# Hybrid SSD/attention layer on one Trainium2 core: attention's negated row maxima from one matmul a head and half, and group norm factors spread by transposes

## The chip, the core and the metric

One core of a Trainium2 chip runs the whole layer as one program. The engines work side by side, each through its own stream of instructions: TensorE (PE in the profile; its weight loads are PEld), VectorE (DVE), ScalarE (ACT), GpSimd (POOL) and SyncE (SP, which here issues most of the DMAs). TensorE writes its results to PSUM, in banks of 128 partitions by 512 float32; VectorE and ScalarE read them there. The metric is the device time of one execution in microseconds, the median of several runs. Lower is better.

## The reference

One layer over 1024 tokens of width 1024. Two branches start from the same normed input: a Mamba-2 state-space branch (SSD, 32 heads of 64 in 4 groups) and a latent attention branch (16 heads, 96 wide for queries and keys, 64 for values). Their outputs are gated and added, projected, and a gated MLP with a short causal convolution follows. What the change touches:

```python
# attention, one head: causal softmax over the keys
s = jnp.einsum('bqhd,bkhd->bhqk', qb, k).astype(jnp.float32) * scale
s = jnp.where(qpos[:, None] >= key_pos[None, :], s, -jnp.inf)
p = jax.nn.softmax(s, axis=-1).astype(v.dtype)
...
# end of the SSD branch: an RMS norm within each group of 512 channels
y = y.reshape(b, l, D_INNER) * jax.nn.silu(z)
y = rms_norm(y.reshape(b, l, SSD_GROUPS, D_INNER // SSD_GROUPS),
             norm_g.reshape(SSD_GROUPS, D_INNER // SSD_GROUPS))
```

All of it is float32 at the boundary. The kernel computes the large products in three passes, with each operand split into a rounded part and a remainder (`mm3`, lines 175 to 177).

## The kernel before

**Order.** PE runs its instructions in program order; at the end of the kernel every PE instruction is chained to the one before it. The other engines' streams follow from the order of the program and its dependencies. While attention and the SSD scan run, PE also works through a queue of background projections: `fill()` and `advance()` put a number of background steps, given by a string of digits (`PACE`), between the steps of the foreground. A background step is one `mm3`, three matmuls of 128x128 by 512 columns into the tile `lin`.

**Attention** (lines 528 to 760, 110 to 690 us in the profile). It goes over 8 pairs of heads and 2 halves of 512 queries. For each pair, half and head:

- `qk_transposed` (L605 to L615) puts queries and keys with the head's dimension on partitions: `qh`, `ql`, `kh`, `kl`. They have 97 rows: 96 of the head and one more, which is 1 in the keys and is to hold the negated row maximum in the queries. So the product of keys and queries comes out with the maximum subtracted.
- `maxima` (L617 to L645) works out that maximum beforehand. For each of 4 blocks of 128 queries PE multiplies queries by keys (L627), and DVE takes the row maximum (L629, L632) into `nm`. DVE then writes the 4 columns of maxima, one for each block of queries, into columns 96 to 99 of the tile `mcol` (L637 or L639, `mc` in the profile), whose first 96 columns are zero. Four matmuls (L643) follow: number i takes columns i to i+96 of `mcol` as its stationary operand and the negated identity `nid` as its moving one, so its row 96 is the negated maxima of block i as a row of 128. One ACT copy (L644) takes row 96 of all four, 512 columns, from PSUM to row 96 of `qh`.
- `key_block` (L647 to L665) multiplies 128 keys by the 512 queries, adds the causal mask on the diagonal (L657, DVE), takes exp (L659, ACT) and adds up the sums; `values` (L670) multiplies by V, two key blocks later.

The heads of a pair go through `maxima` step by step in turn (`both`), so the two L643 blocks of a pair stand one after the other in PE's stream, with background steps between them in four of the 16 pairs. The maxima of a pair's second half are computed while the first half's key blocks run, and those of the next pair's first half while the second half's run; the list `SIDE` says how many such side steps go into each gap. The last two side steps during a first half stand just ahead of that half's end; during a second half there are six more gaps behind them.

The tiles named `s` are four PSUM banks that L627, L643, the key blocks and the transposes take in turn.

**SSD** (lines 832 to 968, 790 to 1275 us). It goes over 4 groups and 8 chunks of 128 tokens. `ssd_inputs` starts a chunk with four transposes (L840) and two matmuls (L842, L844). Group norm is in `ssd_finish`, for each group and half: four matmuls (L947) sum the squares over partitions, `rsqrt_mean` (L123 to L125, DVE) makes 4 columns of factors `rr` (`grr` in the profile), and four float32 matmuls (L955) spread them. Number i takes column i, read 128 times, as its stationary operand and the identity as its moving one, so that every partition of the PSUM tile `np_` gets the 128 factors as a row. DVE then multiplies the four channel tiles by it (L958), and they are stored.

Of the kernel before, what the change touches and what calls it, by code (L numbers as in the profile page):

```python
# [10 lines left out]
F32R = mybir.dt.float32r  # L11
I32 = mybir.dt.int32
AF = mybir.ActivationFunctionType
ALU = mybir.AluOpType
# [3 lines left out]
P = 128  # L18
# [54 lines left out]
def tile_hybrid_layer(ctx: ExitStack, tc: tile.TileContext, x, cols, cons, w_main, w_small, w_uq, w_ukv,  # L73
                      w_ssd, w_mla, w_o, w_up, w_down, out, pace=PACE):
    nc = tc.nc
    V, S, G, PE = nc.vector, nc.scalar, nc.gpsimd, nc.tensor
# [20 lines left out]
    ident = cn[:, CC_ID:CC_ID + 128]  # L97
# [10 lines left out]
    def col(c):  # L108
        return cl[:, c:c + 1]

    def hs_(half):
        return slice(half * 512, half * 512 + 512)

    def rsqrt_mean(dst, ss, n):

        w = dst.shape[1]
        v = const.tile([P, 16], F32, name="rsv", bufs=1)[:, 0:w]
        a = const.tile([P, 16], F32, name="rsa", bufs=1)[:, 0:w]
        V.tensor_scalar(v, ss, 1.0 / n, EPS, op0=ALU.mult, op1=ALU.add)
        V.tensor_scalar(dst.bitcast(I32), v.bitcast(I32), 1, None, op0=ALU.logical_shift_right)  # L120
        V.tensor_scalar(dst.bitcast(I32), dst.bitcast(I32), -1.0, float(0x5F3759DF), op0=ALU.mult, op1=ALU.add)
        for _ in range(3):
            V.scalar_tensor_tensor(a, dst, -0.5, v, op0=ALU.mult, op1=ALU.mult)  # L123
            V.tensor_tensor(a, a, dst, op=ALU.mult)
            V.scalar_tensor_tensor(dst, a, 1.5, dst, op0=ALU.add, op1=ALU.mult)  # L125
# [9 lines left out]
    def last(engine):  # L135
        return [ins for ins in nc.cur_bb.bb.instructions if ins.engine == engine][-1].name
# [15 lines left out]
    def split(raw, hi, lo, eng=None):  # L152
        S.copy(hi, raw)  # L153
        (eng or V).tensor_sub(lo, raw, hi.bitcast(F32))  # L154
# [24 lines left out]
    def act_tile():  # L179
        return hp.tile([P, 2, 512], F32R, name="h")  # L180
# [14 lines left out]
    def lin_tile():  # L195
        return pl.tile([P, 512], F32, name="lin")
# [231 lines left out]
    rr = bp.tile([P, 2, NT], F32, name="lrr")  # L428
# [8 lines left out]
    for half in range(2):  # L437
        for b in range(3):
            fill()
            ps = bps.tile([P, 512], F32, name="tps")  # L440
# [49 lines left out]
    for n in range(17, 1, -2):  # L490
# [10 lines left out]
    ps = bps.tile([P, 512], F32, name="tps")  # L501
    PE.matmul(ps[:, 0:256], lhsT=tri, rhs=va, start=True, stop=True)
    S.copy(acum.rearrange("p t h -> p (t h)"), ps[:, 0:256])
    ps = bps.tile([P, 512], F32, name="tps")
# [9 lines left out]
                           op0=ALU.mult, op1=ALU.mult)  # L514
    act_ = bq.tile([HEADS, T], F32, name="act_")
    for half in range(2):
        fill()
        ps = bps.tile([P, 512], F32, name="tps")
# [7 lines left out]
    with tc.tile_pool(name="cp", bufs=2) as cp, tc.tile_pool(name="pss", bufs=4, space=PSUM) as pss, \  # L526
# [6 lines left out]
        nid = cp.tile([P, P], F32R, name="nid", bufs=1)  # L533
        V.tensor_scalar(nid, ident, -1.0, None, op0=ALU.mult)

        mcol = [cp.tile([P, 100], F32R, name=f"mc{hd}", bufs=1) for hd in range(2)]
        for hd in range(2):
            V.tensor_scalar(mcol[hd][:, 0:96], ident[:, 0:96], 0.0, None, op0=ALU.mult)
        npair = MH // 2
        qkv, qkvT = {}, {}  # L540

# [60 lines left out]
        def bank():  # L602
            return pss.tile([P, 512], F32, name="s")
# [13 lines left out]
        def maxima(pr, half, hd):  # L617

            qh = qkvT[pr, half, hd, "q"][0]
            nm = cp.tile([P, 2, 4], F32, name="nm")  # L620
            for i in range(4):
                n = (i + 1) * P
                for j in range(half + 1):
                    kh = qkvT[pr, j, hd, "k"][0]
                    w = n if j == half else 512
                    ps = bank()
                    PE.matmul(ps[:, 0:w], lhsT=qh[0:96, i * P:(i + 1) * P], rhs=kh[0:96, 0:w], start=True, stop=True)  # L627
                    if j == half:
                        V.tensor_tensor_reduce(ps[:, 0:w], ps[:, 0:w], negw[:, 512 - w:512], 1.0, 2 * NEG,  # L629
                                               ALU.add, ALU.max, nm[:, j, i:i + 1])  # L630
                    else:
                        V.tensor_reduce(nm[:, j, i:i + 1], ps[:, 0:w], axis=AX.X, op=ALU.max)  # L632
                if i < 3:
                    yield
            mc = mcol[hd][:, 96:100]
            if half:
                V.tensor_tensor(mc, nm[:, 0, :], nm[:, 1, :], op=ALU.max)  # L637
            else:
                V.tensor_copy(mc, nm[:, 0, :])  # L639
            yield  # L640
            ps = bank()
            for i in range(4):
                PE.matmul(ps[0:97, i * P:(i + 1) * P], lhsT=mcol[hd][:, i:i + 97], rhs=nid, start=True, stop=True)  # L643
            S.copy(qh[96:97, :], ps[96:97, :])  # L644
            yield  # L645

        def key_block(pr, half, j, hd, accs):  # L647
# [49 lines left out]
        def both(pr, half):  # L697
            a, b = maxima(pr, half, 0), maxima(pr, half, 1)
            for _ in range(5):
                for g in (a, b):  # L700
                    next(g, None)
                    yield
# [69 lines left out]
    with tc.tile_pool(name="dp", bufs=2) as dp, tc.tile_pool(name="psx", bufs=1, space=PSUM) as psx, \  # L772
# [137 lines left out]
        def ssd_squares(g, c):  # L910
            if c % 4 == 0:
                sums[g, c // 4] = dp.tile([P, 512], F32, name="sqs")
            sq = dp.tile([P, 4, P], F32, name="sq_", bufs=1)
            S.activation(sq, chan[g][:, :, c * P:(c + 1) * P], AF.Square)
            G.tensor_tensor(sq[:, 0:2, :], sq[:, 0:2, :], sq[:, 2:4, :], op=ALU.add)
            G.tensor_tensor(sums[g, c // 4][:, (c % 4) * P:(c % 4 + 1) * P], sq[:, 0, :], sq[:, 1, :], op=ALU.add)
            squared[0] = behind(None)
# [21 lines left out]
        def ssd_finish(g, half):  # L939

            x, s = chan[g], hs_(half)
            if half:
                ssd_squares(g, NT - 1)
                yield
            np_ = psy.tile([P, 512], F32, name="np_")
            for i in range(4):
                PE.matmul(np_[:, i:i + 1], lhsT=sums[g, half][:, i * P:(i + 1) * P], rhs=ones[:, 0:1],  # L947
                          start=True, stop=True)
            rr = dp.tile([P, 4], F32, name="grr")
            rsqrt_mean(rr, np_[:, 0:4], 512)  # L950
            yield
            yield
            np_ = psy.tile([P, 512], F32, name="np_")
            for i in range(4):
                PE.matmul(np_[:, i * P:(i + 1) * P], lhsT=rr[:, i:i + 1].broadcast_to([P, P]), rhs=ident,  # L955
                          start=True, stop=True)
            for j in range(4):
                V.scalar_tensor_tensor(x[:, j, s], x[:, j, s], col(CG_SSDG + 4 * g + j), np_,  # L958
                                       op0=ALU.mult, op1=ALU.mult)
                r0 = (4 * g + j) * P  # L960
                if g == GROUPS - 1 and half == 0:
                    t = act_tile()
                    split(x[:, j, s], t[:, 0, :], t[:, 1, :])
                    ya0[4 * g + j] = t
                else:
                    nc.sync.dma_start(out=y_d[r0:r0 + P, s], in_=x[:, j, s])
            if half:
                finished[0] = g + 1
            yield
# [97 lines left out]
        for n, _ in enumerate(conv_group(0)):  # L1067
# [3 lines left out]
            if n == 33:  # L1071
                name = last(mybir.EngineType.DVE)
# [7 lines left out]
        for g in range(GROUPS):  # L1080
            if g + 1 < GROUPS:
                background += [conv_group(g + 1), z_tiles(*((12,), (13,), (14, 15))[g])]
            else:
                background += [mla_tiles()]

            advance(8 if g else 14)
            n = (106, 104, 128, 112)[g]
            for u, _ in enumerate(ssd_steps(g)):
                advance((u + 1) * n // 23 - u * n // 23)
                if (u % 2 or u == 0) and fins and next(fins[0], 0) == 0:  # L1090
                    fins.pop(0)
                if u % 3 == 1 and (g < 2 or g == 2 and u < 5):
                    normalize(8 * g + u // 3)
                if u == 14:
                    fins.append(ssd_finish(g, 0))
            fins.append(ssd_finish(g, 1))
            if g + 1 < GROUPS:
                flush(1 if g < 2 else 0)
                later()
                if g == GROUPS - 2:  # L1100
                    z_load((g + 1) * NT)
# [68 lines left out]
    with tc.tile_pool(name="ep", bufs=2) as ep:  # L1170
        x2b = []
        with tc.tile_pool(name="em", bufs=2) as em:
# [33 lines left out]
            for half in range(2):  # L1206
# [6 lines left out]
                for ct in range(8):  # L1213
# [4 lines left out]
                    if half == 0 and ct == 0:  # L1218
                        ps = head[0]
                    else:  # L1220
                        ps = lin_tile()
# [210 lines left out]
        for k in range(1, 9):  # L1432
# [3 lines left out]
            i = (k - 1) % 4  # L1436
# [343 lines left out]
```

## Time and profile before

| | |
|---|---|
| median of 3 runs | 2205.24 us (2204.86 to 2205.38) |
| span of the profiled execution, first to last instruction | 2202.2 us |
| around the span (median less span) | 3.0 us |
| mean granted TensorE clock | 0.996 |
| L643, L955 matmul records | 128, 64 |
| L644 copies on ACT | 32 |

The profile is of one execution. Its page gives the span and no other time for that execution; what lies around the span is therefore taken from the median of the runs. Busy time is the union of the instructions' durations on an engine. PE's matmuls are pipelined, so their durations overlap (a 512-column matmul is shown as 0.39 us, but the next one starts 0.23 us after it): what an instruction costs PE is read from start to start. In the timeline each row has the start, the time that the group takes, engine, line, operation, what is written and read, sizes and count; a bracket at the end gives the idle time before it and what ended it. `128*97` means 128 rows by 97 columns of a stationary operand.

### The profile page before, as it was taken

What the parts mean: (1) busy time and instruction counts of PE and PEld (TensorE: products, weight loads), DVE (VectorE), ACT (ScalarE), POOL (GpSimd) and SP (SyncE); (2) the same over time, 40 slices, a digit from 0 to 9 for tenths busy, and PEclk for the clock granted to TensorE, in tenths of its full rate; (3) what the DMA queues carried; (4) which work ended last, traced back from release to release, by engine and by line L of the source; (5) the groups of instructions that cost most, each with busy time, mean ns of one, the idle gap of its engine ahead of it and who ended that gap; (6) DMA issues with size and microseconds to landing.
All of it is one profiled execution on the core that took longest, in us unless ns stands there. A gap on an engine that the chain in (4) does not pass through costs nothing. (4 is left out here: it accounts for less than half of the span.)

```text
span 2202.2 us, 30596 instructions
## 1 busy us (share of the span) xinstructions
PE 2151.8 (98%) x10972; PEld 1723.4 (78%) x10972; DVE 1446.8 (66%) x2567; ACT 1050.6 (48%) x1938; POOL 971.3 (44%) x1049
## 2 busy tenths in 40 slices
PE   8999999999999999999999999999899999999999
PEld 6887777777777887878877888887678888877787
DVE  4466756576664469898877745546876676676763
ACT  5445444554444446565654424324745455554330
POOL 2344424432443237665555311003387777744440
PEclk9999999999999999999999999999999999999999
DMA  4221111101112324554366567452132333248642
GB/s 147 69 69 46 40 53 64 50 35 55 64 44 70 115 77 144 176 171 156 115 221 205 169 208 231 160 175 96 63 112 99 110 106 106 95 143 329 257 158 82
DMA packets 121768, 268.99 MB, mean 122 GB/s; under 512 B 13520, under 2 KB 25744, under 8 KB 121616
## 3 DMA queue, kind: packets, MB, share of 16 engines
q1 hardware_dynamic: 105600, 214.47, 28.9%
q0 software_dynamic: 14528, 49.29, 6.7%
q10 hardware_dynamic: 1488, 3.28, 0.4%
q8 instruction: 86, 1.41, 0.3%
q14 instruction: 66, 0.54, 0.1%
HBM read 201.45 MB, written 65.54 MB: 121 GB/s over the span
## 5 line engine op out<-in xcount | busy, mean ns | idle before, releaser
L175 PE MATMUL lin<-h,whi 128*128 128x512 f32 x1440 | 592.3, 411 | 0.5 <-DVE lt L330 0.5
L177 PE MATMUL lin<-h,wlo 128*128 128x512 f32 x1440 | 564.0, 392 | 0.0
L176 PE MATMUL lin<-h,whi 128*128 128x512 f32 x1440 | 562.7, 391 | 0.0
L175 PEld LDWEIGHTS lin<-h,whi 128*128 128x128 f32 x1440 | 271.0, 188 | 83.0 <-issue 34.1
L177 PEld LDWEIGHTS lin<-h,wlo 128*128 128x128 f32 x1440 | 270.5, 188 | 59.9 <-DVE wlo L154 0.4
L176 PEld LDWEIGHTS lin<-h,whi 128*128 128x128 f32 x1440 | 271.7, 189 | 53.7 <-issue 7.0
L154 POOL TENSOR_TENSOR wlo<-wraw,whi 128x512 fp32r<-128x512 f32 x134 | 192.7, 1455 | 164.4 <-ACT whi L153 163.7
L153 ACT CAST whi<-wraw 128x512 fp32r<-128x512 f32 x232 | 141.0, 619 | 258.1 <-PE lin L176 121.0
L664 POOL TENSOR_TENSOR acc<-acc,e 128x512 f32<-128x512 f32 (+3 forms) x80 | 78.6, 983 | 251.0 <-ACT e L659 227.5
L659 ACT ACTIVATE e<-s 128x512 f32<-128x512 f32 (+1 forms) x192 | 93.6, 493 | 168.9 <-DVE s L657 142.8
L1141 DVE TENSOR_TENSOR xlo<-ur,xhi 128x512 fp32r<-128x512 f32 (+1 forms) x41 | 83.2, 2029 | 61.0 <-ACT xhi L1140 61.0
L154 DVE TENSOR_TENSOR wlo<-wraw,whi 128x512 fp32r<-128x512 f32 x98 | 69.8, 722 | 72.1 <-ACT whi L153 71.7
L850 ACT ACTIVATE seg<-abc,acum 128x128 f32<-128x128 f32 x256 | 80.2, 390 | 51.5 <-PE yp L891 43.9
L175 PE MATMUL dps<-tq,h 128*128 128x512 f32 x242 | 97.5, 403 | 6.6 <-DVE xr L1602 3.3
L176 PE MATMUL dps<-tq,h 128*128 128x512 f32 x242 | 97.6, 403 | 0.8 <-DVE tq L154 0.8
L177 PE MATMUL dps<-tq,h 128*128 128x512 f32 x242 | 97.3, 402 | 0.0
L812 DVE SCALAR_TENSOR_TENSOR xg<-craw,cl,xg 128x1024 f32<-128x1024 f32 x48 | 73.8, 1537 | 27.4 <-ACT xg L810 26.9
L664 DVE TENSOR_TENSOR acc<-acc,e 128x512 f32<-128x512 f32 (+3 forms) x80 | 55.0, 688 | 37.6 <-ACT e L659 37.0
L670 PE MATMUL pv<-e,vt 128*64 128x512 f32 (+3 forms) x384 | 72.9, 498 | 0.0
L154 DVE TENSOR_TENSOR h<-ar,h 128x1024 fp32r<-128x1024 f32 (+1 forms) x35 | 56.7, 1623 | 24.5 <-ACT h L153 24.3
L1217 POOL DMA_DIRECT2D mt<-m_d x16 | 8.6, 540 | 144.6 <-DVE gt L1226 96.8
L629 DVE CUSTOM_DVE_ANT_0 s<-s,negw 128x128 f32<-128x128 f32 (+3 forms) x128 | 62.3, 495 | 13.5 <-PE s L627 13.4
(617 smaller groups left out, 5225.6 us busy)
## 6 DMA issues: line engine op xcount, KB each, us to landing
wraw<-in_w_main SPq DMA_DIRECT2D x112, 256.0 KB
ur<-in_w_up SPq DMA_DIRECT2D x44, 512.0 KB
ar<-f_d SPq DMA_DIRECT2D x34, 512.0 KB
abc<-ac_d POOLq DMA_DIRECT2D x32, 512.0 KB, 5.2
wraw<-in_w_ssd SPq DMA_DIRECT2D x64, 256.0 KB
f_d<-wraw POOLq DMA_DIRECT2D x33, 256.0 KB, 2.4
g_d<-lt SPq DMA_DIRECT2D x32, 256.0 KB
z_d<-lt SPq DMA_DIRECT2D x32, 256.0 KB
```

Source lines behind the costliest of these rows:

```text
L153: S.copy(hi, raw)
L154: (eng or V).tensor_sub(lo, raw, hi.bitcast(F32))
L175: PE.matmul(ps, lhsT=ah, rhs=bh, start=first, stop=False, **more)
L176: PE.matmul(ps, lhsT=ah, rhs=bl, start=False, stop=False, **more)
L177: PE.matmul(ps, lhsT=al, rhs=bh, start=False, stop=last, **more)
L629: V.tensor_tensor_reduce(ps[:, 0:w], ps[:, 0:w], negw[:, 512 - w:512], 1.0, 2 * NEG, ALU.add, ALU.max, nm[:, j, i:i + 1])
L659: S.activation(e[:, c0:512], ps[:, 0:w], AF.Exp)
L664: (V if hd else G).tensor_tensor(accs[hd][:, c0:512], accs[hd][:, c0:512], e[:, c0:512], op=ALU.add)
L670: PE.matmul(pv[hd * 64:(hd + 1) * 64, c0:512], lhsT=vt[:, j, hd * 64:(hd + 1) * 64], rhs=es[hd][:, c0:512], start=first, stop=last)
L812: V.scalar_tensor_tensor(c, raw[:, k:k + T], col(cw + k), c, op0=ALU.mult, op1=ALU.add)
L850: S.activation(seg[:, hd, :], abc[:, hd, :], AF.Relu, bias=acum[:, c, 8 * g + hd:8 * g + hd + 1], scale=-1.0)
L1141: eng.tensor_sub(lo, r, hi.bitcast(F32))
```

## The change

Two edits, both on PE's way.

1. `mcol` becomes 128 columns wide and is zeroed as a whole. The 4 columns of maxima go to columns 0, 32, 64 and 96. One matmul with the whole tile as stationary operand gives rows 0, 32, 64 and 96 of its result, the negated maxima of the four blocks of queries. Four ACT copies, each from one of these partitions, 128 columns, fill row 96 of `qh`.
2. The four matmuls that spread the group norm factors become four PE transposes of the same broadcast column.

```diff
-        mcol = [cp.tile([P, 100], F32R, name=f"mc{hd}", bufs=1) for hd in range(2)]
+        mcol = [cp.tile([P, P], F32R, name=f"mc{hd}", bufs=1) for hd in range(2)]
         for hd in range(2):
-            V.tensor_scalar(mcol[hd][:, 0:96], ident[:, 0:96], 0.0, None, op0=ALU.mult)
+            V.tensor_scalar(mcol[hd], ident, 0.0, None, op0=ALU.mult)
...
-            mc = mcol[hd][:, 96:100]
+            mc = mcol[hd][:, 0:P:32]
             if half:
                 V.tensor_tensor(mc, nm[:, 0, :], nm[:, 1, :], op=ALU.max)
             else:
                 V.tensor_copy(mc, nm[:, 0, :])
             yield
             ps = bank()
+            PE.matmul(ps[:, 0:P], lhsT=mcol[hd], rhs=nid, start=True, stop=True)
             for i in range(4):
-                PE.matmul(ps[0:97, i * P:(i + 1) * P], lhsT=mcol[hd][:, i:i + 97], rhs=nid, start=True, stop=True)
-            S.copy(qh[96:97, :], ps[96:97, :])
+                S.copy(qh[96:97, i * P:(i + 1) * P], ps[32 * i:32 * i + 1, 0:P])
             yield
...
             np_ = psy.tile([P, 512], F32, name="np_")
             for i in range(4):
-                PE.matmul(np_[:, i * P:(i + 1) * P], lhsT=rr[:, i:i + 1].broadcast_to([P, P]), rhs=ident,
-                          start=True, stop=True)
+                PE.transpose(np_[:, i * P:(i + 1) * P], rr[:, i:i + 1].broadcast_to([P, P]), ident)
```

## The prediction

> **What bounds the kernel now.** I read the engine row of the page first, then the table by stretches of the two stages that are touched, and then the timeline around the edited lines.
>
> ```profile
> PE 2151.8 (98%) x10972; PEld 1723.4 (78%) x10972; DVE 1446.8 (66%) x2567; ACT 1050.6 (48%) x1938; POOL 971.3 (44%) x1049
> 110.00:690.00 580.00, 569.39 (x3191) 440.17 (x3189) 371.30 (x1025) 278.02 (x628) 228.54 (x384) 1.00 0.16 52
> 790.00:1275.00 485.00, 479.54 (x2896) 385.32 (x2895) 399.23 (x635) 273.29 (x522) 263.34 (x248) 1.00 0.51 165
> ```
>
> In the stretch rows the columns are length, then busy time of PE, PEld, DVE, ACT and POOL, then granted clock, DMA share and GB/s. PE is busy for 569.4 of 580 us while attention runs and for 479.5 of 485 us in the state-space stage (SSD), at full clock; DMA is busy for 16% and 51%. PE issues in program order, so a microsecond of PE taken out of either stage shortens the run by a microsecond, unless PE then waits for what it did not have to wait for.
>
> **What leaves PE: the maxima.** The pairs of blocks L643 (head 0, head 1) appear in two shapes: eight matmuls in one row, or four and four with a triple of background matmuls between.
>
> ```profile
> 384.58 0.39 PE L177 MATMUL lin<-h,wlo 128*128 128x512 f32 x1
> 384.81 0.82 PE L643 MATMUL s<-nid,mc 128*97 128x128 f32 x8
> 385.38 1.06 ACT L644 CAST qh<-s 1x512 fp32r<-1x512 f32 x2 [0.37 <-PE s L643]
> 385.98 0.40 PE L177 MATMUL lin<-h,wlo 128*128 128x512 f32 x1
> 386.22 0.40 PE L175 MATMUL s<-qh,kh 97*128 97x512 f32 x1
> ```
> ```profile
> 309.12 0.39 PE L177 MATMUL lin<-h,wlo 128*128 128x512 f32 x1
> 309.36 0.48 PE L643 MATMUL s<-nid,mc 128*97 128x128 f32 x4
> 309.67 0.45 PE L175 MATMUL lin<-h,whi 128*128 128x512 f32 x1
> 310.19 0.40 PE L177 MATMUL lin<-h,wlo 128*128 128x512 f32 x1
> ```
> ```profile
> 882.39 0.39 PE L175 MATMUL lin<-h,whi 128*128 128x512 f32 x1
> 882.62 0.39 PE L176 MATMUL lin<-h,whi 128*128 128x512 f32 x1
> 882.84 0.39 PE L177 MATMUL lin<-h,wlo 128*128 128x512 f32 x1
> 883.07 1.05 PE L955 MATMUL np__8996<-cn,grr 128*128 128x128 f32 x8
> 883.96 0.60 PE L840 MATMUL xp<-cn,xg 128*128 128x128 f32 x4
> 884.39 0.39 PE L842 MATMUL sp<-chan 128*128 128x128 f32 x2
> ```
>
> Durations overlap, so I use starts. A 512-column background step is 0.23 us (882.39, 882.62, 882.84, 883.07). From L177 to the next L177 there are three such steps, 0.68 us; with eight L643 between it is 385.98-384.58 = 1.40, so eight cost 0.72; with four, 310.19-309.12 = 1.07, so four cost 0.39. The difference, 0.33 for four, is 0.083 us for each. Of the 32 blocks, 12 pairs are of the first shape and 4 of the second. After the change a pair is two matmuls. The edge of a block stays: 0.39-3x0.083 = 0.14 for one matmul, and 0.22 for two. The new stationary tile has 128 columns, not 97; no row shows that form with 128 moving columns alone, and the nearest rows are these 0.083 and the 0.11 us of a transpose with 128 (L840, 884.39-883.96 = 0.43 for four). I take 0.02 more for each block, nearly the whole of that difference: 0.16 for one, 0.24 for two. So a pair of the first shape saves 0.48 us and one of the second 0.46, about 0.25 in the first block and 0.23 in the second; 12x0.48+4x0.46 = 7.6 us, and 8.0 without the 0.02.
>
> The Trainium skill ("TensorE: Matmul & The Clock Gate", LDWEIGHTS) says that a weight load takes its column count over 1.2 GHz, however many rows it has; that speaks against the edit a little, as 97 columns become 128. As an estimate by that page, 81 ns become 107 ns. The rows give 83 ns a matmul with 97 columns, close to it, and by the rule the edit would save 4x81-107 = 217 ns a block, 6.9 us in all.
>
> **Where this is lost again before head 1's block.** Head 1's matmul needs its own maxima from DVE.
>
> ```profile
> 161.15 0.39 PE L177 MATMUL lin<-h,wlo 128*128 128x512 f32 x1
> 161.20 0.47 DVE L637 TENSOR_TENSOR mc<-nm 128x4 fp32r<-128x4 f32 x1
> 161.38 0.28 ACT L659 ACTIVATE e<-s 128x128 f32<-128x128 f32 x1 [1.49 <-DVE s L657]
> 161.38 0.90 PE L643 MATMUL s<-nid,mc 128*97 128x128 f32 x8
> 161.95 1.06 ACT L644 CAST qh<-s 1x512 fp32r<-1x512 f32 x2 [0.30 <-PE s L643]
> 162.63 0.40 PE L177 MATMUL lin<-h,wlo 128*128 128x512 f32 x1
> 162.87 0.40 PE L175 MATMUL s<-qh,kh 97*128 97x512 f32 x1
> ```
> ```profile
> 503.81 0.17 DVE L639 CAST mc<-nm 128x4 fp32r<-128x4 f32 x1
> 504.12 0.53 PE L643 MATMUL s<-nid,mc 128*97 128x128 f32 x4 [0.40 <-DVE mc L639]
> ```
>
> At 161 the second `mc` ends at 161.67, and four first-head matmuls of 0.083 have just gone by (161.38 plus 0.33): remove three of them, and PE waits that 0.25 us. At 504 it waits already. Going through the 16 pairs in the same way, six are like these two (the first and the last of them are shown): the first block's 0.25 is lost. Three more have the second `mc` only 0.2 to 0.3 us ahead and lose 0.3 together. That takes 6x0.25+0.3 = 1.8 from 7.6 and leaves 5.8. DVE's work is upstream and does not change: the strided write of `mc` has as many elements, and the wider zeroing at the start of attention is two instructions once.
>
> **What is added on ACT: four copies for one.** 32 copies of 512 columns become 128 of 128 columns, on one partition each. No row has 1x128; the nearest in length are 128x128 from PSUM.
>
> ```profile
> 165.54 0.27 ACT L567 COPY vt<-s 128x128 f32<-128x128 f32 x1 [0.43 <-DVE qk L566]
> 165.71 0.61 ACT L659 ACTIVATE e<-s 128x512 f32<-128x512 f32 x1
> ```
>
> Such a copy is 0.27 us long, and the next instruction starts 0.17 us after it. Four in a row are 3x0.17+0.27 = 0.78, and I take that, the nearest row, against 0.58 for the one copy now (two take 1.06, so the second starts 0.48 after the first). The bounds are 0.58 (no more than the one copy, as the columns are the same in all) and 3x0.48+0.27 = 1.71 (the step of the copies that are there). ACT as a whole has room: 278 of 580 us busy, and 96 more steps of 0.17 are 16 us. What queues behind the copies is the next exp (L659), used two key blocks later, so that hides. The copies themselves matter where the key block that reads `qh` row 96 comes at once. After a second half's maxima (eight pairs) PE has other key blocks to run first; the closest reader starts 4.4 us after its copy:
>
> ```profile
> 652.69 1.06 ACT L644 CAST qh<-s 1x512 fp32r<-1x512 f32 x2
> ...
> 657.06 0.45 PE L175 MATMUL s<-qh,kh 97*128 97x512 f32 x1
> ```
>
> After a first half's maxima (eight pairs) it has only what the views show:
>
> - 161: the result now reaches ACT after one matmul, 161.38+0.34 = 161.72 (0.34 is the wait from the last of the four, 161.61, to 161.95). Copies end at 162.50, the reader can start 0.07 later (as at 461 below), 162.57, and PE arrives at 162.87-0.23 = 162.64. Nothing is lost. One more pair looks the same.
> - 384: copies from 385.15 to 385.93, reader at 386.00; PE arrives at 386.22-0.48 = 385.74. Lost: 0.26.
> - Two where ACT is held by an exp and PE already waits for the copy:
>
> ```profile
> 460.33 0.28 ACT L659 ACTIVATE e<-s 128x128 f32<-128x128 f32 x1 [1.91 <-DVE s L657]
> 460.64 1.06 ACT L644 CAST qh<-s 1x512 fp32r<-1x512 f32 x2
> 461.29 0.48 PE L175 MATMUL s<-qh,kh 97*128 97x512 f32 x1
> ```
> ```profile
> 532.98 0.28 ACT L659 ACTIVATE e<-s 128x128 f32<-128x128 f32 x1 [2.57 <-DVE s L657]
> 533.28 1.06 ACT L644 CAST qh<-s 1x512 fp32r<-1x512 f32 x2
> 533.91 0.51 PE L175 MATMUL s<-qh,kh 97*128 97x512 f32 x1
> ```
>
> Here the exp comes from DVE and does not move, the copies end 0.2 later than now, and the reader starts 0.2 later: 461.5 and 534.1. The savings of both pairs (0.23 and 0.3) are lost and 0.2 on top: 0.43 and 0.5. The last three have a background triple more between, or an earlier copy, and 1 us of room: nothing.
>
> Together 1.2. Attention keeps 5.8-1.2 = 4.6 us.
>
> **Group norm factors by transposes.** A float32 matmul L955 is two records here, 883.96-883.07 = 0.89 for four; the transposes L840 right behind it, of the same tile size, are one record each and take 0.43. Both load a 128x128 stationary tile and move the identity. So 0.455 us a group, 8 groups, 3.65 us. The new stationary operand is a column read 128 times, as it is in L955 now; no row shows a transpose of such a read, so its cost is bounded by 0.43 and by 0.89 (nothing gained); I take 0.43, the row of the same operation.
>
> ```profile
> L958 DVE SCALAR_TENSOR_TENSOR xg<-xg,cl,np__8996 x4: 735/735/735, 888.4 to 890.3; 128x512 f32<-128x512 f32 x4
> ```
> ```profile
> PE sn L874 <- DVE bt L863: 4.3, 3, 2.3
> ```
>
> DVE reads the factors of 883 only at 888.4, so it gains nothing and loses nothing there. PE keeps the gain unless DVE makes it wait; DVE is busy for 399 of 485 us, but PE's waits for it here are 4.3 us in three places (`bt`), each some 20 us or more behind an L955 and ended by DVE work that PE released in between, so they move with PE.
>
> **The sum.** 4.6+3.65 = 8.25 us off the span of 2202.2, which gives 2193.95. The median of the runs, 2205.24, lies 3.0 above this span; with that the forecast is **2197.0**.
>
> **The rivals.**
>
> *All hidden*: one-partition copies are cheaper, and the waits for `mc` dissolve because DVE is released earlier. Then 7.6+3.65 = 11.25 are saved: 2194.0. For it: ACT and DVE have idle time. Against: PE already waits at 504, 460 and 533.
>
> *The transposes gain nothing*: the repeated column or the transpose mode costs a second pass. 2205.2-4.6 = 2200.6. Against it stands the L840 row at 0.11 us each. The Trainium skill ("TensorE: Matmul & The Clock Gate", Part 4) says that the full clock does not engage for transposes, as they do not count as busy; at half clock four would take 0.87, and the gain would be gone in this way too. The trace disagrees: the clock is 1.00 over the stretch that holds these L840.
>
> *The copies cost 0.48 a step*, as today's do. Four then end 0.93 later than I assumed. Worked through as above, the eight tight readers wait 0.9, 0.9, 0.5, 1.2, 1.4, 1.5, 0.5 and 0.2 us, and the last head 1 reader 1 more, 8 us in all; attention loses 2.2, the transposes bring 3.65, and 1.4 is left: 2203.8, no change that can be measured.
>
> *Slower*: the copies run one after another without overlap, each 0.58. Four take 2.3 for each head; at the eight tight places head 0's reader waits 0.6 longer than in the last case and head 1's too, about 17 us in all against 5.8+3.65 = 9.45 saved: 2212.8. It decides from a step of about 0.5 us on, where the loss passes 9.45. Against it: 0.17 in the row of L567, and even today's copies overlap.
>
> **How the numbers follow.** Forecast 60% (its own range 2194.5 to 2199.5); all hidden 12%; transposes without gain 8%; copies at 0.48, 13%; slower 7%. The range takes the first three with the ends of their prices: from 2193.5 (8.0+3.65 = 11.65) to 2202.0 (transposes without gain, and 1.4 more for the copies). About 0.2%, 4.4 us, is what a measurement of this kernel can tell from no change. Faster: 0.60+0.12+0.08 = 0.80; within: 0.13; slower: 0.07.
>
> **What would show it.** L643: 32 matmuls, and 0.15 or 0.25 us a block by starts. L644: four copies in 0.78 us. PE waiting for `qh` L644 at three or four first-half ends, under 0.6 each. The transposes: four records in 0.43, eight times. The attention stretch 4.6 us shorter, SSD 3.6. It is wrong if steps of ACT's copies near 0.5 appear, if the planner puts other ACT work between the copies, or if new waits of PE appear elsewhere.

## The result, and the profile after

| | before | after |
|---|---|---|
| median (lowest to highest) of 17 runs each, us | 2205.38 (2201.22 to 2208.77) | 2200.39 (2196.48 to 2205.16) |
| ratio of the two, 95% interval | | 0.9977 (0.9969 to 0.9986) |
| span of the profiled execution, us | 2202.2 | 2201.3 |
| time of that execution, us | not given | 2203.12 |

The changed kernel is 5.0 us faster (0.0023 x 2205.4; by the interval 3.1 to 6.8). The forecast was 2197.0, 8.25 us faster. The two profiled spans differ by 0.9 us only. The profiled execution of after is 2.7 us above its own median, and that of before below its own: where a run's time and its span are both given, as here, 1.8 us (2203.12 - 2201.3) lie around the span, so before's took about 2204.0. Two spans alone would have said that almost nothing happened.

In the code after, the maxima are L642, the copies L644 and the transposes L955 as before, and the multiplication by the factors, behind them, is L957.

The engine row and the attention stretch of after, to be read against those of before (length, then busy time of PE, PEld, DVE, ACT and POOL, granted clock, DMA share, GB/s):

```profile
PE 2145.3 (97%) x10844; PEld 1713.8 (78%) x10844; DVE 1446.8 (66%) x2567; ACT 1064.3 (48%) x2034; POOL 969.6 (44%) x1049
```
```profile
110.00:690.00 580.00, 567.72 (x3113) 434.76 (x3112) 371.86 (x1026) 294.12 (x727) 229.72 (x385) 1.00 0.16 52
```

128 records are gone from PE (10972 to 10844: 96 in the maxima, 32 in the group norm) and 96 copies more are on ACT, which is busy for 16.1 us more in attention (278.0 to 294.1). This window stands still while the work in it moves up. What a stage gained is read from its landmarks instead, in rows of one line and tile (count, duration in ns, first to last start). Before, then after:

```profile
L610 PE MATMUL s<-cn,qk x256: 270/272/352, 119.1 to 663.6; 128*97 128x128 f32 x128
L840 PE MATMUL xp<-cn,xg x128: 270/272/310, 795.4 to 1238.3; 128*128 128x128 f32 x128
L955 PE MATMUL np__12753<-cn,grr x8: 275/275/347, 1265.7 to 1266.6; 128*128 128x128 f32 x8
```
```profile
L610 PE MATMUL s<-cn,qk x256: 270/272/351, 119.1 to 660.5; 128*97 128x128 f32 x128
L840 PE MATMUL xp<-cn,xg x128: 270/272/310, 791.6 to 1231.8; 128*128 128x128 f32 x128
L955 PE MATMUL np__12753<-cn,grr x4: 272/273/295, 1260.3 to 1260.7; 128*128 128x128 f32 x4
```

From the first L610, at 119.1 in both, to the first L840 the program is 3.9 us ahead (676.36 against 672.42; the rows above round to tenths; forecast 4.6). At the last L955 of all it is 1266.6 - 1260.7 = 5.9 ahead, of which the SSD stage brought 2.0 (forecast 3.65). The rest of the program, whose code is the same, then took 5.1 us longer in this one profile, which leaves the difference of the two spans. How much of that is scatter takes more profiles, below.

The timeline around 384 us, the place that the prediction worked through, now reads (start, time, engine, line, operation; in brackets the idle time before and what ended it):

```profile
384.11 0.40 PE L177 MATMUL lin<-h,wlo 128*128 128x512 f32 x1
384.34 0.33 PE L642 MATMUL s<-nid,mc 128*128 128x128 f32 x2
384.51 0.45 PE L175 MATMUL lin<-h,whi 128*128 128x512 f32 x1
...
384.66 1.87 ACT L644 CAST qh<-s 1x128 fp32r<-1x128 f32 x7
385.03 0.39 PE L177 MATMUL lin<-h,wlo 128*128 128x512 f32 x1
385.77 0.50 PE L175 MATMUL s<-qh,kh 97*128 97x512 f32 x1 [0.35 <-ACT qh L644]
```

From L177 to the next L177 it is 385.03 - 384.11 = 0.92, against 1.40 before: the pair saves the 0.48 of the forecast. But from that first L177 to the key block that reads `qh` it is 385.77 - 384.11 = 1.66, against 386.22 - 384.58 = 1.64 before. The whole saving goes into a wait for the copies. The ACT row holds seven copies in 1.87 us; one alone is 0.256, so they start (1.87 - 0.256)/6 = 0.27 us apart, each after the end of the last, where the forecast had 0.17 with an overlap.

The group norm behind 879 us:

```profile
878.93 0.39 PE L177 MATMUL lin<-h,wlo 128*128 128x512 f32 x1
879.15 0.60 PE L955 MATMUL np__8996<-cn,grr 128*128 128x128 f32 x4
879.59 0.60 PE L840 MATMUL xp<-cn,xg 128*128 128x128 f32 x4
```

Four transposes, four records, 879.59 - 879.15 = 0.44 us against 0.89: the repeated column costs nothing extra, and the 0.43 of the forecast held.

### The profile page after: what moved, and what is told of

It reads as the page before. It is cut to its first block, busy times and chain, and to the rows that moved or that the text cites. A ratio compares the mean times of both kernels' runs of the same rounds, so it can differ in the third digit from the quotient of the medians.

```text
span 2201.3 us, 30448 instructions
## 1 busy us (share of the span) xinstructions
PE 2145.3 (97%) x10844; PEld 1713.8 (78%) x10844; DVE 1446.8 (66%) x2567; ACT 1064.3 (48%) x2034; POOL 969.6 (44%) x1049
## 5 line engine op out<-in xcount | busy, mean ns | idle before, releaser
L177 PE MATMUL lin<-h,wlo 128*128 128x512 f32 x1440 | 563.7, 391 | 0.0
L177 PEld LDWEIGHTS lin<-h,wlo 128*128 128x128 f32 x1440 | 270.4, 188 | 59.8 <-POOL wlo L154 0.4
L177 PE MATMUL dps<-tq,h 128*128 128x512 f32 x242 | 96.4, 398 | 0.0
L629 DVE CUSTOM_DVE_ANT_0 s<-s,negw 128x128 f32<-128x128 f32 (+3 forms) x128 | 62.3, 495 | 13.5 <-PE s L627 13.4
```

The lines of the kernel that those rows point to most:

```text
L177: PE.matmul(ps, lhsT=al, rhs=bh, start=False, stop=last, **more)
```

## The experiments

The theory after this reading: both edits do on PE what the prediction says; what is missing goes into PE's waits, for the copies in attention (a step of 0.27, not 0.17) and for DVE in the SSD stage. The rivals: one edit brings nothing; the step belongs to the order or the partitions of the copies and can be mended; or the missing part is scatter. Each ratio is to executions of the kernel before on the same chip, with its 95% interval; it can differ from the quotient of the two medians, here by up to 0.0008.

**Each edit alone.** The first has edit 1 only, the second edit 2 only.

> The first edit alone: one matmul and four copies for the maxima, group norm factors spread by matmuls as before. Theory: PE gains 5.9 us in the L643 blocks and loses 2.0 us again where key blocks wait for the last of the four copies, so PE is 3.9 us ahead of the kernel before at the end of attention and stays 3.9 ahead through the SSD stage; the time is 3 to 4 us lower. Rival: the copies eat the gain, PE is less than 1 us ahead at the end of attention and the time is the same.

> The second edit alone: group norm factors by transposes, maxima as before. Theory: nothing moves in attention; each of the eight groups of four takes 0.44 us less of PE, and some of it comes back as waits for DVE, so PE is 2.6 to 3.5 us ahead at the end of the SSD stage; the time is 2 to 3.5 us lower. Rival: DVE sets the pace of the SSD stage, PE waits longer for it by what it gained, and PE is less than 1 us ahead at the end of that stage.

Edit 1 alone: 2204.30 against 2206.13, ratio 0.9992 (0.9983 to 1.0002). Edit 2 alone: 2204.62, ratio 0.9998 (0.9989 to 1.0006). Neither can be told from no change by its time. Their landmarks say more. From the first L610 to the last L955 the three profiles of before (in the table below) take 1147.7 us on average; the kernel with edit 1 alone is 2.5 us ahead of that, of 3.9 expected, and the one with edit 2 alone 0.9, of 2.6 to 3.5 expected. Waits of PE from 790 to 1275 us, in the kernel with edit 1 alone (what waits, for what; us in total, times, longest), then in that with edit 2 alone, then after:

```profile
PE sn L874 <- DVE bt L863: 5.4, 3, 3.4
PE np__12753 L955 <- DVE grr L125: 1.0, 1, 1.0
PE lin L175 <- DVE lt L330: 0.9, 1, 0.9
```
```profile
PE sn L874 <- DVE bt L863: 4.4, 3, 2.2
PE lin L175 <- DVE lt L330: 1.9, 1, 1.9
PE np__12753 L955 <- DVE grr L125: 1.1, 1, 1.1
PE yp L891 <- DVE seg L864: 0.8, 2, 0.6
```
```profile
PE sn L874 <- DVE bt L863: 4.4, 3, 2.3
PE np__12753 L955 <- DVE grr L125: 1.8, 1, 1.8
PE lin L175 <- DVE lt L330: 1.5, 1, 1.5
PE yp L891 <- DVE seg L864: 0.8, 2, 0.5
```

The wait of L891 for `seg` is in every kernel that has the transposes and in none that hasn't. The waits for `bt` stay as they were, as forecast, except that they are 1.1 us longer with edit 1 alone. Here is why the one for `seg` appears: DVE's timeline before, and below it what PE does at the same place.

```profile
887.04 1.41 DVE L817 SCALAR_TENSOR_TENSOR xg<-craw,xg 128x1024 f32<-128x1024 f32 x1
888.37 2.71 DVE L958 SCALAR_TENSOR_TENSOR xg<-xg,cl,np__8996 128x512 f32<-128x512 f32 x4
891.00 0.28 DVE L847 SCALAR_TENSOR_TENSOR sm__9025<-sp,cn 128x128 f32<-128x128 f32 x1
891.20 0.68 DVE L855 TENSOR_TENSOR xdt<-xp,dtt 128x512 f32<-128x512 f32 x1
891.80 1.21 DVE L864 TENSOR_TENSOR seg<-seg,sm__9025 128x1024 f32<-128x1024 f32 x1
```
```profile
892.67 0.39 PE L177 MATMUL lin<-h,wlo 128*128 128x512 f32 x1
893.15 0.44 PE L891 MATMUL yp<-seg,xdt 128*64 128x128 f32 x4
```

DVE works without a gap here. It was running behind, and it doesn't wait for PE: the factors lie ready from 883.96 and are read from 888.37 on. `seg` ends at 891.80 + 1.21 = 893.01 and L891 starts 0.14 later. Where nothing waits, L891 starts 0.32 behind the L177 ahead of it (1003.85 to 1004.17, for one), which would be 892.99. So DVE ended last already, by 0.16 us that show no bracket. After the change:

```profile
887.87 1.21 DVE L864 TENSOR_TENSOR seg<-seg,sm__9025 128x1024 f32<-128x1024 f32 x1
```
```profile
888.29 0.39 PE L177 MATMUL lin<-h,wlo 128*128 128x512 f32 x1
889.23 0.44 PE L891 MATMUL yp<-seg,xdt 128*64 128x128 f32 x4 [0.55 <-DVE seg L864]
```

DVE is 3.93 us earlier than before, which is what attention had brought (PE reached L955 3.92 earlier, 883.07 to 879.15). PE's last background matmul is 4.38 earlier, but L891 again 3.92. The 0.46 that this group had gained is lost. Behind the third group, at 1000 us, it happens again, in part: before, `seg` ended at 1003.94 and was 0.1 us early for the L891 at 1004.17; after, L891 waits, and 0.33 of the gain is lost.

From the first L840 to the fifth group's first L955, that is over four groups, all profiles agree: 320.8 to 320.9 us in the four with matmuls, 319.9 to 320.0 in the nine with transposes and nothing else changed in the SSD stage. So four groups bring 0.9 us, half of 4 x 0.44.

**How much of the copies' price is paid.** One of the four copies is left.

```diff
-            for i in range(4):
-                S.copy(qh[96:97, i * P:(i + 1) * P], ps[32 * i:32 * i + 1, 0:P])
+            S.copy(qh[96:97, 0:P], ps[0:1, 0:P])
...
-            S.activation(e[:, c0:512], ps[:, 0:w], AF.Exp)
+            S.activation(e[:, c0:512], ps[:, 0:w], AF.Exp, scale=0.1)
```

> Both edits, but three of the four copies are left out: only the first 128 of 512 columns of the maxima reach the queries, and exp is taken of a tenth of the score so that it stays finite. Theory: the 2 us that key blocks wait at the ends of first halves are the length of the row of four copies (1.06 us with 0.27 from start to start, against 0.58 of the one copy before); with one copy of 0.26 they vanish, PE is 5.5 to 6.2 us ahead of the kernel before at the end of attention, and the time is about 2 us below that with both edits. Rival: the reader waits for the exp that holds ACT, or for the signal from PE, and not for the copies; then PE is 4 us ahead, as with four copies.

2196.29, ratio 0.9963 (0.9950 to 0.9976), so 8.2 us below the kernel before (5.3 to 11.0) where both edits whole give 5.0. This kernel leaves out three quarters of the maxima and serves for its time alone. No key block waits for `qh` any more; what is left of waits for copies is ahead of maxima matmuls, twice:

```profile
PEld s L642 <- ACT qh L643: 1.5, 2, 0.7
```

The copies take back some of what PE gains. The times put that at 3 us, with intervals that overlap, the landmarks at 1.5 in attention; the waits show the direction, and the size is known only to about this.

**Two engines for the copies.** The second and the fourth go to DVE.

```diff
-                S.copy(qh[96:97, i * P:(i + 1) * P], ps[32 * i:32 * i + 1, 0:P])
+                (V.tensor_copy if i % 2 else S.copy)(qh[96:97, i * P:(i + 1) * P], ps[32 * i:32 * i + 1, 0:P])
```

> Both edits, with two of the four copies on ACT and two on DVE. Theory: each engine's two copies take about 0.53 us and run side by side, the reader waits about 0.5 us less at each of the five tight ends, PE is 5 to 6 us ahead of the kernel before at the end of attention, and the time is 1 to 2 us below that with both edits. Rival: DVE's copies queue behind DVE's other work (its sums of exp, its masks), PE gains nothing over four copies on ACT or loses.

2204.93, ratio 0.9994 (0.9985 to 1.0003): the gain is gone. PE's and PEld's waits, and one place of the timeline:

```profile
PE s L175 <- DVE qh L644: 2.6, 5, 0.8
PEld s L175 <- DVE qh L644: 6.3, 9, 1.3
```
```profile
160.92 0.25 ACT L644 CAST qh<-s 1x128 fp32r<-1x128 f32 x1
161.24 1.33 DVE L644 CAST qh<-s 1x128 fp32r<-1x128 f32 x4
161.38 0.86 ACT L644 CAST qh<-s 1x128 fp32r<-1x128 f32 x3 [0.21 <-PE s L642]
162.34 0.50 PE L175 MATMUL s<-qh,kh 97*128 97x512 f32 x1 [0.28 <-DVE qh L644]
```

The two engines go in turn rather than side by side: the first DVE copy starts at 161.24, only after the first ACT copy has ended at 161.17, though it writes other columns. Each handing over costs a wait: a head's next copy, on the other engine, starts only when the one before it has ended. Whether DVE's other work delays them too isn't shown.

**Is the order of the partitions the cause?**

```diff
-            for i in range(4):
+            for i in (0, 2, 1, 3):
```

> Both edits, the four copies in the order 0, 2, 1, 3. With two engines the two ACT copies of blocks 0 and 2 went 0.16 us from start to start; in the order 0, 1, 2, 3 on ACT alone the step is 0.27. Theory: the step is 0.27 where a copy writes the 128 columns next to those of the copy before it; then 0 to 2 and 1 to 3 take 0.16, the four copies take 0.85 or less in place of 1.06, and the waits for them fall from 2.0 to 1.2 to 1.5 us. Rival: a copy on ACT alone takes 0.27 from start to start in any order, and nothing moves.

2198.67, ratio 0.9972 (0.9960 to 0.9984), the same as after. ACT's timeline:

```profile
160.03 2.15 ACT L644 CAST qh<-s 1x128 fp32r<-1x128 f32 x8
```

Eight copies in 2.15: (2.15 - 0.256)/7 = 0.27 again. The step doesn't depend on this order.

The 0.16 us that this experiment started from had been read wrongly. In the kernel with two engines the two ACT copies at 384 us start at 383.67 and 383.83, and DVE's copies at 383.95 and 384.17, each just after one of them has ended: they are the first copies of head 0 and of head 1, and not blocks 0 and 2 of one head. The kernel with one copy a head has the same pair:

```profile
381.87 0.41 ACT L643 CAST qh<-s 1x128 fp32r<-1x128 f32 x2
```

Two copies take 0.41 us and one alone 0.253, so the second starts 0.16 after the first, close to the 0.17 of the forecast. The 0.27 therefore doesn't belong to the shape 1x128 but to a row of four copies for one head. After such a row the next head's first copy comes without overlap too (385.46 to 385.74 in after, with a wait for an ACT copy). What keeps the copies of a row apart isn't shown, and the two heads' copies in turn on ACT alone weren't tried.

**More room ahead of the readers.** The last two side steps of a first half, the maxima and their copies among them, move up, by a whole step or by half of one.

```diff
-        SIDE = [[1, 1, 1, 1, 1, 1, 1, 1, 2, 2, 2, 2], [1] * 10 + [0] * 1 + [2] * 7 + [0] * 6]
+        SIDE = [[1, 1, 1, 1, 1, 1, 2, 2, 2, 2, 0, 2], [1] * 10 + [0] * 1 + [2] * 7 + [0] * 6]
```
```diff
+        SIDE = [[1, 1, 1, 1, 1, 1, 1, 2, 2, 2, 1, 2], [1] * 10 + [0] * 1 + [2] * 7 + [0] * 6]
```

> Both edits, and the maxima of a second half are worked out one gap earlier, so that a key block and a triple of background matmuls stand between the copies and their reader. Theory: the 2 us of waits for the copies vanish, PE is 5.5 to 6.5 us ahead of the kernel before at the end of attention against 4, and the time is about 2 us below that with both edits. Rival: DVE gets less time for the maxima, PE waits for it ahead of the L642 matmuls by as much as it no longer waits for the copies, and the time is the same.

> Both edits, and the maxima of a second half come half a gap earlier: head 0's block and its copies one gap ahead of where they are, head 1's where it is. Theory: the reader that waits is head 0's, so PE's waits for the copies fall from 4.0 to below 1 us, DVE's part moves too little to add waits, attention is 1 to 2 us shorter than with both edits (672.5 us from the first transpose of attention to the first of the SSD stage), and the time is 1 to 2 us lower. Rival: as with a full gap, PE's waits for DVE's maxima (L627 for its bank) grow by as much, and attention is as long.

2199.70, ratio 0.9971 (0.9960 to 0.9982), and 2201.61, ratio 0.9978 (0.9970 to 0.9987): both the same as after. PEld's waits from 110 to 690 us, after, then with the whole step, then with half:

```profile
PEld s L175 <- ACT qh L644: 3.2, 6, 0.9
PEld s L627 <- ACT e L659: 2.4, 6, 0.6
PEld s L627 <- DVE nm L632: 1.5, 7, 0.4
```
```profile
PEld s L627 <- DVE nm L632: 3.1, 12, 0.4
PEld s L627 <- ACT e L659: 2.9, 8, 0.5
PEld s L175 <- ACT qh L644: 0.4, 1, 0.4
```
```profile
PEld s L627 <- ACT e L659: 5.2, 13, 0.6
PEld s L627 <- DVE nm L629: 2.8, 6, 0.6
```

The waits for the copies go from 3.2 to 0.4 with the whole step, and the two kinds of L627 grow from 3.9 to 6.0. With half a step 1.2 is left for the copies, and L627 waits 5.2 for exps and 2.8 for L629. L627 writes an `s` bank that the key blocks, the maxima and the transposes share; two side steps in one gap take banks that the last reader, an exp or a row maximum, has not yet let go. The stall moved, and the stage got no shorter (first L610 to first L840 takes 673.0 and 673.1 us, and 672.4 to 673.5 in three profiles of after).

**The waits for `bt`.** The copy of `bt` moves from DVE to ACT, to see whether DVE's lateness in the SSD stage can be bought off.

```diff
+            bt = None
+            if c < NT - 1:
+                bt = dp.tile([P, P], F32, name="bt")
+                S.copy(bt, sp[:, 256:384])
...
-            xde = bt = None
+            xde = None
...
-                bt = dp.tile([P, P], F32, name="bt")
-                V.tensor_copy(bt, sp[:, 256:384])
```

> Both edits, and the copy of the transposed B tile (bt, 31 copies of 0.28 us) goes from DVE to ACT, ahead of ACT's decay work of the same chunk. Theory: in the SSD stage PE loses part of the transposes' 3.5 us because DVE is late (0.8 us more at L891 for seg, 4.4 us at L874 for bt); with 8.7 us less on DVE and bt no longer behind it, these waits fall by 2 us or more and the SSD stage is 2 us or more shorter than with both edits (469 us on average). Rival: ACT then waits for PE's transposes in the middle of its own queue, decay comes later, and the stage is no shorter or longer.

2203.57, ratio 0.9994 (0.9984 to 1.0004): the gain of the edits can no longer be told from nothing. PE's waits in the SSD stage (lines stand two higher here):

```profile
PE sn L876 <- ACT bt L849: 3.2, 2, 3.0
PE sn L876 <- DVE xde L864: 2.6, 1, 2.6
...
PE sn L876 <- DVE grr L125: 1.2, 1, 1.2
PE yp L893 <- DVE seg L866: 0.8, 2, 0.4
```

4.4 us for `bt` became 3.2 + 2.6 + 1.2 for `bt` on ACT, `xde` and the factors. The wait for `seg` is untouched: in DVE's timeline above, no copy of `bt` stands between the factors and `seg`.

**Both kernels again.** Unchanged, for scatter.

> The changed kernel once more, for its time beside the others and a second profile. Theory: up to the end of the SSD stage PE is ahead by the same 6 to 6.5 us as in the first profile, within 1 us, and what it is ahead at the last instruction differs by 2 us or more between the two profiles, as the stages behind 1260 us vary from one execution to the next. Rival: the stages behind 1260 us give back 5 us again, as in the first profile, because a transfer there does not start earlier.

> The kernel before once more, for a second profile. Theory: behind 1260 us it stands 2 us or more off its own first profile, in one direction or the other, with no edit at all; up to the end of attention it is within 1 us of it. Rival: it repeats its first profile within 1 us throughout, and what the changed kernel loses behind 1260 us is a consequence of the edits.

> The changed kernel a third time, for a profile. Theory: the stages behind the last group norm block, 935 to 937 us in three profiles without the first edit and 940 to 942 in five of seven with it, vary by chance; 935 to 942 can come here. Rival: the first edit shifts them, and it is 940 or more again.

> The kernel before a third time, for a profile. Theory: the stages behind the last group norm block vary by chance and can take 935 to 942 us here. Rival: without the first edit they take 935 to 937 us again.

After again: 2200.51, ratio 0.9972 (0.9961 to 0.9984), and one execution at 2199.82; before, one each at 2206.40 and 2204.82, beside medians of 2205.54 and 2205.19. The result repeats. The landmarks of the profiles of each kernel, worked out as above (us; "rest" is from the last L955 to the end of the span):

| | first L610 to first L840 | to the last L955 | rest |
|---|---|---|---|
| before, three profiles | 676.4, 677.2, 676.3 | 471.1, 471.9, 470.2 | 935.6, 936.5, 938.4 |
| transposes alone | 676.5 | 470.3 | 936.8 |
| maxima alone | 672.2 | 473.0 | 942.1 |
| after, three profiles | 672.4, 673.5, 672.8 | 469.1, 470.5, 470.1 | 940.7, 941.5, 937.8 |
| after, other order of copies | 672.1 | 468.2 | 940.2 |
| one copy | 671.1 | 468.3 | 934.6 |
| copies on two engines | 676.2 | 468.3 | 940.5 |
| maxima a step, half a step earlier | 673.0, 673.1 | 471.1, 468.6 | 936.0, 939.3 |
| `bt` on ACT | 673.4 | 471.7 | 937.7 |

The first column separates cleanly: 676.6 us as the mean of the four profiles without edit 1, 672.6 of the five with it (maxima alone, after, other order), so edit 1 brings 4.0. The second has more scatter: 471.5 without the transposes (before three times, maxima alone), 469.6 with them (transposes alone, after three times, other order), so 1.9. In the third, whose code is the same everywhere, single profiles lie between 934.6 and 942.1. From matmul to matmul the traces show where: over about half of this rest PE's stream repeats to 0.1 us, and most of the differences lie in three stretches of before's time: from 1323 to 1381 us, where PE waits for split weights (`whi`, `wlo`; 56.8 to 58.6 us in the four profiles without edit 1, 56.7 to 60.2 in the ten with it), from 1493 to 1614, and from 1959 to 2090.

## Why the prediction was right or wrong

The direction was right, and the measured time, 2200.4, lies inside the range of 2193.5 to 2202.0. It lies outside the forecast's own range of 2194.5 to 2199.5, and the gain of 8.25 is outside the measured interval of 3.1 to 6.8. The wider range reaches that far for a rival, the transposes that gain nothing (2200.6), and that is not what happened. Most of the missing part is found, in two terms.

- **What leaves PE in the maxima: right.** Where nothing waits a pair saves 0.46 to 0.52 us, where head 1's `mc` ends last 0.21 to 0.33; together 5.9 us against 5.8. That the totals agree so well is luck: at 431 a wait of 0.57 for `mc` is gone that the prediction had left standing, and at 356 one of 0.75 is new. The second stands in this profile alone; in three others with the same maxima (edit 1 alone, after again and a third time) the total is about 6.7. The stationary tile of 128 columns costs no more than assumed. By the rule of the Trainium skill ("TensorE: Matmul & The Clock Gate", LDWEIGHTS) a pair would have saved 0.43, twice the 0.217 estimated from it; the measured 0.46 to 0.52 are nearer to the price from the rows.
- **The copies: mechanism right, size wrong.** The step was taken as 0.17 us from an ACT copy of 128x128 followed by an exp; in a row of four for one head it is 0.27, though two heads' single copies do start 0.16 apart. Four copies take 3 x 0.267 + 0.256 = 1.06, not 0.78. PE then waits at five of the eight first-half ends, where the prediction's sum had three: at 161 and its like it had no loss and there is about 0.3 at each; at 384 it had 0.26 and there is 0.5; at 460 0.16 for 0.43. At 532 an exp got in between the first copy and the others, which the prediction named as a way to be wrong, and the loss is 0.6 for 0.5. Together about 1.9 us for 1.2.
- **Attention as a whole.** 5.9 - 1.9 = 4.0 in the first profile, whose landmarks show 3.9; the mean over the profiles is 4.0, for 4.6. Where the maxima bring 6.7, other small waits take the difference back; a part is at 144 us, where an L610 comes some 0.5 us later, behind an exp.
- **The transposes: right as an operation, wrong as a stage.** 0.44 to 0.45 a group, 3.5 us in all, for 3.65. The step that failed is that "PE keeps the gain unless DVE makes it wait", with only `bt` looked at, and that DVE "gains nothing and loses nothing". DVE was running without a gap behind two of the eight groups; for L891 it already ended last by 0.16 us at the one and had 0.1 to spare at the other, so little of what PE gains there counts. That is 0.8 us. Behind the fifth group, at 1141 us before and 1137 after, a background matmul waits for `lt` L330: 0.3, 1.0, none and 0.9 us in the four profiles without the transposes, 1.9, 1.5, 1.9, 1.8 and 1.2 with them (alone, after three times, other order), 1.1 more on average. ACT makes `lt` just behind a copy that waits for a weight transfer (`wraw<-in_w_mla`, 2.84 us in the first profile of before, 3.38 in the first of after), so the transfer ends last there. But with the copies on two engines, and the same transposes, there is no such wait; how much of the 1.1 is the change and how much the scatter of the transfer isn't shown. The landmarks keep 1.9.
- **What lies around the span.** The 3.0 us were the median less the span of a run that was faster than its median; around the span of a run with both numbers it is 1.8. The difference to before was used, so this costs the forecast nothing, but it hid that one profile is one draw from runs that spread over 8 us.
- **The rivals.** "All hidden" is out, "transposes gain nothing" is out as an operation (0.11 us each at a granted clock of 1.00), but about half of that loss came about in another way. The two dearer prices of the copies, 0.48 and 0.58, are out.

With the measured terms the sum is 5.9 - 1.9 + 3.5 - 0.8 = 6.7 us, just inside the measured interval of 3.1 to 6.8; the wait for `lt` can take up to 1.1 from it. The landmarks up to the last L955 give 4.0 + 1.9 = 5.9, well inside. What stays open is the 0.9 us between that and the 5.0 of the medians. The landmarks would have it in the rest of the program: the ten profiles with edit 1 average 939.0 there, the four without 936.8. But the ten reach from 934.6 to 942.1 and the four from 935.6 to 938.4, and they overlap; whether the change costs something there, or single profiles scatter so, these runs don't settle, and no cause is named.

## What to carry to other kernels

Merging matmuls and paying for it with small copies is worth the saving on PE only where the first reader has slack for the whole chain of copies; measure the step of a copy of just that shape, in just such a row, before counting on an overlap. When an instruction leaves the bounding engine, check, place by place behind it, whether another engine runs without a gap and already ends last at the next meeting point, where an idle time of 0.2 us shows as nothing but a start that is late by that much. Moving work earlier doesn't remove a stall where the place it moves to is short of buffers: 2.8 us of waits for the copies went, and 2.1 us of waits for banks came.

## What the hardware showed that was not expected

A copy of 1x128 from PSUM takes 0.256 us on ACT, scarcely less than one of 128x128 (0.27), and in a row of four for one head the next starts 0.267 after it, with no overlap, in whichever of two orders the source partitions come. Where each head has a single copy, the second head's did overlap the first's by 0.1 us: 0.16 apart at 1x128, 0.48 apart at 1x512 (1.06 for two).

Part of the scatter between executions goes with the granted clock. Of the executions of the kernel before that stood beside these experiments, 8 with a mean granted clock of 0.994 took 2207.8 us on average and 9 with 0.998 took 2203.8; a lower clock by 0.4% would by itself be 8.8 us at most, and 4.0 are seen. In the profiles single groups of matmuls show a doubled step (0.43 for 0.23 us) at places that differ from one execution to the next.
